# A two-block model in one kernel: the order of the even layer's mixers, their small operations, and where the modulation starts

## The chip, the cores and the metric

The kernel runs on one core of a Trainium2 chip, one launch. Times are device microseconds of that core. The time before is the median of three runs, 827.32 us (826.36 to 827.43). The engines are TensorE (PE; its weight loads are PEld), VectorE (DVE), ScalarE (ACT), GpSimd (POOL) and SyncE (SP), whose queue issues nearly all DMAs. TensorE's clock has two levels, 1.2 and 2.4 GHz; the profile shows the granted share of the higher.

## The reference

All tensors are float32; one sequence of 256 tokens, width 1024. The first block has two layers, x = x + layer(rms_norm(x)). The even one projects to mixers' columns, runs mLSTM (4 heads of 128) on one part and a sparse attention (8 heads of 64 in 2 groups) on the other, and projects back:

```python
proj = h @ w_in + b_in
ya = mlstm_branch(m_cols, ...)   # softmax-free attention with running gates, rms norm, * sigmoid(o) * silu(z)
yb = nsa_branch(n_cols, ...)     # (gated sum of compressed, selected and window attention) * silu(z)
return concatenate([ya, yb]) @ w_out
```

The odd layer is a gated recurrence (HGRN). The second block has a pooling layer and a spatial gating layer, each followed by an MLP of width 4096; every norm there is modulated by vectors that come from c:

```python
c_act = silu(c)
mod = c_act @ ada_w[i] + ada_b[i]          # 1024 x 6144, for each of two layers
sh1, sc1, g1, sh2, sc2, g2 = split(mod, 6)
h = rmsnorm(x, norm_mix_g[i]) * (1 + sc1) + sh1
```

## The kernel before

Activations lie transposed, features on partitions and the 256 tokens in the free dimension. Every large product is made at nearly fp32 accuracy from three fp32r matmuls: weights and activations are split into a high and a low part. Weights come by DMA as `raw` tiles of 128x2048 (1 MB, three buffers, two pieces of 1024 columns); `split_w` (L155 to L163) makes of a piece `whi`, a cast on ScalarE (L161), and `wlo`, a subtraction on VectorE (L162), four buffers each. `tile_T` (L190) then issues 24 matmuls (L221 to L223), eight k-steps of three; `tiles_tok` (L195; L206 to L208) is the same with tokens on the output's partitions and up to 512 columns. An output is evicted by `norm.scaled` (L310 to L313), a product with the norm's reciprocal root on VectorE, and what its kind wants.

The program is unrolled in Python. A scheduler puts each engine's instructions in order by priority, which is the place in the program, and by what it reckons to be ready; `tc.high_priority(offset=n)` moves an instruction's place n ahead, or back if n is negative. On the chip each engine keeps that order and waits at semaphores.

The even layer (`even_layer`, L404) works through 35 column tiles in the order of `EV_TILES` (L27): compress keys and values, the attention's keys and queries, gates G, values, then mLSTM's v, q and k, the gates mo, mz and nz. Between groups of tiles it advances two generators: `nsa` (L610: compress, query and key norms, then eight steps of attention, one per query block and head pair) and `mlstm` (L534: gates, four heads, a joint norm). The last attention step is run after mz3 and before nz0 (L527). Then out_proj (L315) runs eight tiles over the pairs `y` into xT. At L766 the attention's exponent takes scale 0.125 and a bias that L764 makes from the maximum.

An mLSTM head h spreads the rows `mr` and `bc` (4 heads by 256 tokens, fp32) over 128 partitions by a matmul with a one-hot column of the identity:

```python
sel = ident[0:4, h : h + 1].to_broadcast([4, 128])
PE.matmul(pb[:, 0:T], sel, mr, start=True, stop=False)
PE.matmul(pb[:, 0:128], ident_bf, mneg_bf, start=False, stop=True)
```

An fp32 matmul shows in the trace as two instructions.

`ada` (L340) makes the modulation vectors on VectorE: 96 loads of 128x1024 (`araw`, 512 KB, two buffers) and 96 reductions with the row c (L353). A step is one or two of them; `step(upto)` (L373) issues the next if fewer than 6 x upto are done, 50 places back in priority, so that they fill gaps. Before, steps start at L517 (`early`, in the mixers), at every second tile of the first out_proj (`every=2`), then in the odd layer and the MLPs; `finish` (L380) sets how many must be done at a point. silu of c is made at L509 to L512 by a tanh, after the first parts of nsa and mlstm, in an `araw` buffer.

`Norm.square` (L283) sums the squares of x over eight feature tiles on VectorE and adds over partitions by a ones-matmul; with `two` the eighth is given to a matmul of its own instead of the sum. Before, `two` holds where a norm has no shift.

Of the kernel before, what the change touches and what calls it, by code (L numbers as in the profile page):

```python
# [65 lines left out]
def tile_kernel(ctx: ExitStack, tc: tile.TileContext, io: dict, out: bass.AP):  # L66
# [82 lines left out]

    def load_raw(src, n=2048):  # L150
        raw = mk(wpool, [128, 2048], F32, "raw", bufs=3)
        nc.sync.dma_start(raw[:, :n], src)
        return raw

    def split_w(raw, piece, halves=False):  # L155

        hi = mk(wpool, [128, 1024], F32R, "whi", bufs=4)
        lo = mk(wpool, [128, 1024], F32R, "wlo", bufs=4)
        r = raw[:, piece * 1024 : (piece + 1) * 1024]
        for c in [slice(0, 1024)] if not halves else [slice(0, 512), slice(512, 1024)]:  # L160
            S.copy(hi[:, c], r[:, c])  # L161
            V.tensor_sub(lo[:, c], r[:, c], hi[:, c])  # L162
        return hi, lo  # L163
# [91 lines left out]
    class Norm:  # L255
# [3 lines left out]
        def __init__(self, gain=None, shift=None):  # L259
            self.gain, self.acc, self.ps, self.pair = gain, None, None, None  # L260
            if gain is not None:
                self.pair = Pair(0 if shift is None else 2)
            self.shift = shift
# [19 lines left out]
        def square(self, k, i=None):  # L283
            i = k if i is None else i
            sq = mk(tmp, [128, T], F32, "sq", bufs=3)
            S.activation(sq, xT[:, k, :], AF.Square)  # L286
            two = self.shift is None
            if i < KT - 1 or not two:
                if self.acc is not None:
                    V.tensor_tensor(sq, sq, self.acc, op=ALU.add)  # L290
                self.acc = sq
                if i < KT - 1 - two:
                    return
                self.ps = mbank()[:, :T]
# [20 lines left out]
    def out_proj(src, pair, evict, side=0, every=1):  # L315
        w = Weights(lambda c: src[c])
        for n in range(8):
            if every and n % every == 0:
                step(side)
            ps = gbank()[:, :T]  # L320
            tile_T(ps, w, n, pair)
            evict(n, ps)
# [81 lines left out]
    def even_layer(norm, nxt, w):  # L404
        with ExitStack() as es:
# [18 lines left out]
            def evict(name, ps):  # L424
# [25 lines left out]
                elif kind == "nz":  # L450

                    V.tensor_scalar(t, t, b, None, op0=ALU.add)
                    z = mk(et, [128, T], F32, "w1", bufs=4)
                    V.tensor_scalar(z, t, -80.0, None, op0=ALU.max)
# [3 lines left out]
                    V.tensor_tensor(nout[:, i, :], nout[:, i, :], t, op=ALU.mult)  # L458
# [43 lines left out]
            columns(EV_TILES[6:11])  # L502
# [5 lines left out]

            th = mk(wpool, [128, 1024], F32, "araw", bufs=2)  # L509
            tanh(th, crow, scale=0.5)  # L510
            V.scalar_tensor_tensor(crow, th, 1.0, crow, op0=ALU.add, op1=ALU.mult)
            V.tensor_scalar(crow, crow, 0.5, None, op0=ALU.mult)  # L512
            side.append(ada(crow))
# [18 lines left out]
            out_proj(io["ev_w_out"], y, add_x(nxt), 5, 2)  # L532

    def mlstm(ev, et, qk, v, gsb, num, tanh):  # L534
# [18 lines left out]
        V.tensor_scalar(mr, mr, -1.0, None, op0=ALU.mult)  # L553
        acol = mk(ev, [128, 2, H], F32, "acol")
# [7 lines left out]
        for h in range(H):  # L562
# [28 lines left out]
            PE.matmul(pm[:, 0:T], sel, bc, start=True, stop=True)  # L591
# [18 lines left out]
    def nsa(ev, et, nqk, sv, gsb, cpair, nout):  # L610
# [64 lines left out]
        gains = lambda i: P("q_norm") if i < 4 else P("k_norm", i - 3)  # L675
# [16 lines left out]
        V.memset(kcb, 0.0)  # L692
        for g in range(2):
            V.tensor_copy(kcb[64 * g : 64 * g + 64, g, :], kcmp[64 * g : 64 * g + 64, 0, :])

        hid4 = mk(et, [128, 2, 4, 32], F32, "w1", bufs=4)
        V.memset(hid4, 0.0)
        V.tensor_copy(hid4[:, :, :, 0:16], hid[:, 1, :, None, :].to_broadcast([128, 2, 4, 16]))
        vcp = mk(ev, [128, 2, 4, 64], F32, "vcp")
        V.memset(vcp, 0.0)  # L700
# [3 lines left out]
        for r in range(4):  # L704
            V.tensor_copy(vcp[32 * r : 32 * r + 32, :, r, :], ps[32 * r : 32 * r + 32, 0:128].rearrange("p (g e) -> p g e", g=2))
# [16 lines left out]
        for qb in range(2):  # L722
# [3 lines left out]
            mx = mk(et, [128, 4, 2, 2], F32, "nmx")  # L726
# [13 lines left out]
            V.memset(ec, 0.0)  # L740
            ecv = ec.rearrange("p g r n -> p (g r) n")[:, :, 0:15]
            V.tensor_tensor(ecv, pcv, mxc[:, :, None].to_broadcast([128, 8, 15]), op=ALU.subtract)
            S.activation(ecv, ecv, AF.Exp, scale=0.125)
# [12 lines left out]
            for j in range(4):  # L756
                E = mk(ev, [128, 2, 2, n], F32, "A", bufs=2)
                for g in range(2):
# [4 lines left out]
                    V.tensor_reduce(mx[:, j, g, :], pv, axis=AX.X, op=ALU.max)  # L763
                    V.tensor_scalar(nmx[:, j, g, :], mx[:, j, g, :], -0.125, None, op0=ALU.mult)  # L764
                    for b in range(2):
                        S.activation(E[:, g, b, :], pv[:, b, :], AF.Exp, bias=nmx[:, j, g, b : b + 1], scale=0.125,  # L766
# [415 lines left out]
    norm = Norm(mods[1][1][:, 0:8], mods[1][0][:, 0:8])  # L1182
    mlp(0, mod, mid, norm)
    mod, gains = mods[1]
    mid = Norm(gains[:, 8:16], mod[:, 24:32])
# [186 lines left out]
```

## Time and profile before

| | |
|---|---|
| median of three runs | 827.32 us |
| the profiled execution's own time | 825.35 us |
| its span, first to last instruction | 823.5 us |
| mean granted clock of TensorE | 0.99 |
| matmul, VectorE, ScalarE busy | 97%, 81%, 63% |
| instructions | 16419 |

The even layer lasts from the start to some 210 us of the span, the odd layer to about 350, the pool layer to about 372, the MLPs and the gating layer to the end. A busy share is the union of an engine's instructions; matmuls overlap in it. In the rows, "x4" is a count, "<-" names what ended a wait, and a line like L162 can be that of a helper used all over the program.

### The profile page before, as it was taken

The numbers are of one execution on the slowest core, as the hardware profiler recorded it, in microseconds if no ns is written. First come the engines' busy times: TensorE is split into PE (matmuls) and PEld (weight loads), VectorE is DVE, ScalarE is ACT, GpSimd is POOL, SyncE is SP. The second block draws the span as 40 slices with busy tenths as digits, with TensorE's granted clock in tenths as the row PEclk, the third lists the DMA queues.
The fourth block names the chain that finished last, engine by engine and source line by source line (L and its number), as shares of the span: only waits on it lengthen the run. The fifth ranks groups of instructions, "written<-read, shape, count | busy, mean of one in ns | idle before, by whom it ended". The sixth has DMA issues, their size and how long they took to land.

```text
span 823.5 us, 16419 instructions
## 1 busy us (share of the span) xinstructions
PE 802.5 (97%) x6568; PEld 739.9 (90%) x6568; DVE 670.8 (81%) x1260; ACT 519.7 (63%) x932; POOL 4.9 (1%) x19
## 2 busy tenths in 40 slices
PE   8999999998999999998999999999999999999996
PEld 7969987888999987998999988889999999988885
DVE  7689988899999999998999988756679877755552
ACT  6656765686876565756877734446657877754441
POOL 0000000001000000000000000000000000000000
PEclk8999999999999999999999999999999999999999
DMA  9644566657885677747989888654446655555521
GB/s 353 244 165 148 179 215 229 228 191 258 301 288 214 245 253 262 232 174 284 345 283 320 304 294 310 245 201 154 168 152 234 221 199 166 193 190 174 199 103 52
DMA packets 34636, 184.66 MB, mean 224 GB/s; under 512 B 3968, under 2 KB 4608, under 8 KB 19200
## 3 DMA queue, kind: packets, MB, share of 16 engines
q1 hardware_dynamic: 33696, 181.96, 62.8%
q10 hardware_dynamic: 864, 1.65, 0.6%
q8 instruction: 52, 0.85, 0.4%
q14 instruction: 24, 0.20, 0.1%
HBM read 182.55 MB, written 1.05 MB: 223 GB/s over the span
## 4 chain that ended last, share of the span: by engine, by line
PE 68%; DVE 15%; DMA 8%; ACT 4%; issue 4%; ACTq 0%; DVEq 0%; SPq 0%
PE g L221 13%; PE g L223 12%; PE g L222 12%; PE g L1057 10%; DMA araw<-in_ada_w_dram 7%; DVE wlo L162 5%; PE g L1058 5%; DVE araw L353 3%; PE m L871 1%; ACT whi L161 1%; PE m L761 1%; DVE nt L312 1%; PE g L207 1%; PE g L208 1%; PE g L206 1%
## 5 line engine op out<-in xcount | busy, mean ns | idle before, releaser
L221 PE MATMUL g<-ahi,whi 128*128 128x258 f32 (+1 forms) x1256 | 359.3, 288 | 8.1 <-ACT ahi L213 3.3
L222 PE MATMUL g<-alo,whi 128*128 128x258 f32 (+1 forms) x1256 | 357.5, 286 | 0.1
L223 PE MATMUL g<-ahi,wlo 128*128 128x258 f32 (+1 forms) x1256 | 356.7, 285 | 0.3 <-DVE wlo L162 0.2
L162 DVE TENSOR_TENSOR wlo<-raw,whi 128x1024 fp32r<-128x1024 f32 (+1 forms) x238 | 288.7, 1216 | 79.9 <-ACT whi L161 79.2
L161 ACT CAST whi<-raw 128x1024 fp32r<-128x1024 f32 (+1 forms) x238 | 246.5, 1043 | 166.8 <-PE g L222 67.0
L221 PEld LDWEIGHTS g<-ahi,whi 128*128 128x128 f32 x1256 | 238.7, 191 | 12.7 <-ACT ahi L213 4.1
L222 PEld LDWEIGHTS g<-alo,whi 128*128 128x128 f32 x1256 | 240.0, 191 | 2.1 <-issue 0.8
L223 PEld LDWEIGHTS g<-ahi,wlo 128*128 128x128 f32 x1256 | 239.3, 191 | 2.1 <-issue 1.0
L1057 PE MATMUL g<-ghl,whi 128*128 128x512 f32 x480 | 168.2, 393 | 0.0
L353 DVE CUSTOM_DVE_ANT_0 araw<-araw,row_c,prm 128x1024 f32<-128x1024 f32 x96 | 122.4, 1278 | 18.0 <-DMA araw<-in_ada_w_dram 17.9
L1058 PE MATMUL g<-ghl,wlo 128*128 128x256 f32 x480 | 134.1, 279 | 0.6 <-DVE wlo L162 0.6
L1057 PEld LDWEIGHTS g<-ghl,whi 128*128 128x128 f32 x480 | 89.9, 187 | 21.2
L1058 PEld LDWEIGHTS g<-ghl,wlo 128*128 128x128 f32 x480 | 89.9, 187 | 1.2 <-DVE wlo L162 1.2
L312 DVE TENSOR_TENSOR nt<-g,nrstd 128x256 f32<-128x256 f32 x133 | 55.5, 418 | 15.1 <-PE g L223 14.3
L1039 ACT ACTIVATE nt<-nt,nb 128x256 f32<-128x256 f32 x64 | 32.4, 507 | 23.5 <-DVE nb L1038 23.5
L280 ACT ACTIVATE ahi<-xT,gains 128x256 fp32r<-128x256 f32 x32 | 16.2, 505 | 23.6 <-DVE xT L332 22.2
L286 ACT ACTIVATE sq<-xT 128x256 f32<-128x256 f32 x56 | 22.3, 404 | 10.6 <-DVE xT L332 10.6
L214 DVE TENSOR_TENSOR ghl<-nt,ghl 128x256 fp32r<-128x256 f32 x64 | 26.9, 422 | 2.2 <-ACT ghl L213 0.2
L1040 ACT ACTIVATE nt<-nt 128x256 f32<-128x256 f32 x64 | 26.7, 418 | 1.9
L213 ACT CAST ghl<-nt 128x256 fp32r<-128x256 f32 x64 | 25.9, 406 | 1.8
L208 PE MATMUL g<-wlo,ahi 128*128 128x512 f32 (+1 forms) x64 | 24.3, 379 | 0.0
L206 PE MATMUL g<-whi,ahi 128*128 128x512 f32 (+1 forms) x64 | 24.2, 378 | 0.0
(302 smaller groups left out, 803.1 us busy)
## 6 DMA issues: line engine op xcount, KB each, us to landing
raw<-in_mlp_w_dram SPq DMA_DIRECT2D x64, 1024.0 KB, 5.0
araw<-in_ada_w_dram SPq DMA_DIRECT2D x96, 512.0 KB, 4.9
raw<-in_ev_w_in_dram SPq DMA_DIRECT2D x17, 1024.0 KB, 5.5
raw<-in_od_w_in_dram SPq DMA_DIRECT2D x16, 1024.0 KB, 5.2
raw<-in_sgu_w_in_dram SPq DMA_DIRECT2D x8, 1024.0 KB, 4.9
raw<-in_ev_w_out_dram SPq DMA_DIRECT2D x4, 1024.0 KB, 4.9
raw<-in_od_w_out_dram SPq DMA_DIRECT2D x4, 1024.0 KB, 4.8
raw<-in_sgu_w_out_dram SPq DMA_DIRECT2D x4, 1024.0 KB, 4.8
```

The source lines that it names most:

```text
L161: S.copy(hi[:, c], r[:, c])
L162: V.tensor_sub(lo[:, c], r[:, c], hi[:, c])
L206: PE.matmul(ps[tb], pair.hi(k)[:, ts_], wh[:, j, :], start=st, stop=False)
L208: PE.matmul(ps[tb], pair.hi(k)[:, ts_], wl[:, j, :], start=False, stop=sp)
L221: PE.matmul(ps, wh(k), ah(k), start=st, stop=False)
L222: PE.matmul(ps, wh(k), al(k), start=False, stop=False)
L223: PE.matmul(ps, wl(k), ah(k), start=False, stop=sp)
L312: V.tensor_tensor(t, ps[:, :T], self.r, op=ALU.mult)
L353: V.tensor_tensor_reduce(raw, raw, crow, 1.0, P("ada_b", layer * 48 + c), ALU.mult, ALU.add, mod[:, c : c + 1])
L1039: S.activation(r, r, AF.Relu, bias=b)
L1057: PE.matmul(ps, wh[:, k, :], a.rearrange("p s t -> p (s t)"), start=st, stop=sp, skip_group_check=True)
L1058: PE.matmul(ps[:, :T], wl[:, k, :], a[:, 0, :], start=False, stop=sp, skip_group_check=True)
```

## The change

Splits of weights get 80 places of priority from the seventh tile of the even layer to the end of its out_proj (`lead`). silu of c is made by exp, ln and exp right before the seventh tile, and one ada step follows each of the tiles 7 to 11. out_proj's steps move to n = 3, 5, 7. The last attention step is run after mo3, ahead of mz0. In mLSTM the rows are split into a high and a low fp32r part in one tile `rows` (partitions 0 to 3 and 32 to 35), and a stationary `two` adds both; the 256 and the 128 columns of `mr` become one product of 384, the two masks one of 256. In the attention the 0.125 goes into the query gain, the negation into the reduction; memsets go from VectorE to GpSimd and small copies from VectorE to ScalarE. nz saves one VectorE operation. The pool layer's second norm is now one with `two`.

```diff
+    lead = [0]
@@ split_w
-        for c in [slice(0, 1024)] if not halves else [slice(0, 512), slice(512, 1024)]:
-            S.copy(hi[:, c], r[:, c])
-            V.tensor_sub(lo[:, c], r[:, c], hi[:, c])
+        with tc.high_priority(offset=lead[0]):
+            for c in [slice(0, 1024)] if not halves else [slice(0, 512), slice(512, 1024)]:
+                S.copy(hi[:, c], r[:, c])
+                V.tensor_sub(lo[:, c], r[:, c], hi[:, c])
@@ Norm
-        def __init__(self, gain=None, shift=None):
+        def __init__(self, gain=None, shift=None, two=True):
...
-            two = self.shift is None
+            two = self.two
@@ out_proj
-            if every and n % every == 0:
+            if every and n % every == every - 1 and n > 1:
                 step(side)
@@ evict, nz
-                    V.tensor_scalar(t, t, b, None, op0=ALU.add)
                     z = mk(et, [128, T], F32, "w1", bufs=4)
-                    V.tensor_scalar(z, t, -80.0, None, op0=ALU.max)
+                    V.tensor_scalar(z, t, b, -80.0, op0=ALU.add, op1=ALU.max)
...
-                    V.tensor_tensor(nout[:, i, :], nout[:, i, :], t, op=ALU.mult)
+                    V.scalar_tensor_tensor(nout[:, i, :], t, b, nout[:, i, :], op0=ALU.add, op1=ALU.mult)
@@ even_layer
             crow = bcast_rows(base, "c")
-            columns(EV_TILES[6:11])
+            lead[0] = 80
+
+            th = mk(wpool, [128, 1024], F32, "araw", bufs=2)
+            V.tensor_scalar(th, crow, -80.0, None, op0=ALU.max)
+            tab[0].activation(th, th, AF.Exp, scale=-1.0)
+            tab[0].activation(th, th, AF.Ln, bias=1.0)
+            tab[0].activation(th, th, AF.Exp, scale=-1.0)
+            V.tensor_tensor(crow, crow, th, op=ALU.mult)
+            side.append(ada(crow))
+            for name in EV_TILES[6:11]:
+                columns([name])
+                step(1)
...
-            th = mk(wpool, [128, 1024], F32, "araw", bufs=2)
-            tanh(th, crow, scale=0.5)
-            V.scalar_tensor_tensor(crow, th, 1.0, crow, op0=ALU.add, op1=ALU.mult)
-            V.tensor_scalar(crow, crow, 0.5, None, op0=ALU.mult)
-            side.append(ada(crow))
...
-            columns(EV_TILES[25:31])
+            columns(EV_TILES[25:27])
+            run(ns)
+            columns(EV_TILES[27:31])
             tab[0] = Table(EXP_LN, tab[0])
             run(ml)
-            run(ns)
...
             out_proj(io["ev_w_out"], y, add_x(nxt), 5, 2)
+            lead[0] = 0
@@ mlstm
+        rows = mk(ev, [128, 640], F32R, "rows")
+        G.memset(rows.bitcast(U32), 0)
+        for c, r in ((slice(0, 256), mr), (slice(256, 384), mr[:, 128:256]), (slice(384, 640), bc)):
+            S.copy(rows[0:4, c], r)
+            V.tensor_sub(rows[32:36, c], r, rows[0:4, c])
+        two = mk(ev, [128, H], F32R, "two")
+        V.tensor_tensor(two, ident[:, 0:4], ident[:, 32:36], op=ALU.add)
...
-            sel = ident[0:4, h : h + 1].to_broadcast([4, 128])
+            sel = two[:, h : h + 1].to_broadcast([128, 128])
             pb = mbank(1)
-            PE.matmul(pb[:, 0:T], sel, mr, start=True, stop=False)
-            PE.matmul(pb[:, 0:128], ident_bf, mneg_bf, start=False, stop=True)
-            PE.matmul(pb[:, 256:384], sel, mr[:, 128:256], start=True, stop=False)
-            PE.matmul(pb[:, 256:384], ident_bf, mneg_bf, start=False, stop=True)
+            PE.matmul(pb[:, 0:384], sel, rows[:, 0:384], start=True, stop=False, skip_group_check=True)
+            diag = pb.rearrange("p (s t) -> p s t", s=2)[:, :, 0:128]
+            PE.matmul(diag, ident_bf, mneg_bf[:, None, :].to_broadcast([128, 2, 128]), start=False, stop=True, skip_group_check=True)
...
-            PE.matmul(pm[:, 0:T], sel, bc, start=True, stop=True)
+            PE.matmul(pm[:, 0:T], sel, rows[:, 384:640], start=True, stop=True)
@@ nsa
+        qg = mk(ev, [128, 1], F32, "qgain")
+        S.mul(qg, P("q_norm"), 0.125)
...
-        V.memset(kblk, 0.0)
+        G.memset(kblk, 0.0)
         for g in range(2):
-            V.tensor_copy(kblk[64 * g : 64 * g + 64, g, :, :], nqk[64 * g : 64 * g + 64, 4:6, :])
+            S.copy(kblk[64 * g : 64 * g + 64, g, :, :], nqk[64 * g : 64 * g + 64, 4:6, :])
...
-                    V.tensor_reduce(mx[:, j, g, :], pv, axis=AX.X, op=ALU.max)
-                    V.tensor_scalar(nmx[:, j, g, :], mx[:, j, g, :], -0.125, None, op0=ALU.mult)
+                    V.tensor_reduce(nmx[:, j, g, :], pv, axis=AX.X, op=ALU.max, negate=True)
```

Left out are the same moves for `kcb`, `hid4`, `vcp` and `ec` (memsets to GpSimd; the copies into `kcb` and `vcp` to ScalarE), the scale 0.125 gone from both exponents, and `False` for `two` written at the gating layer's two norms, which keeps them as they were.

## Rows read from the trace of the kernel before

**Rows 1.** the page, part 1: busy time, share of the span, instructions

```profile
PE 802.5 (97%) x6568; PEld 739.9 (90%) x6568; DVE 670.8 (81%) x1260; ACT 519.7 (63%) x932; POOL 4.9 (1%) x19
```

**Rows 2.** windows: stretch, length, busy us by engine, granted clock, DMA share, GB/s

```profile
29.00:54.00 25.00, 23.60 (x211) 20.04 (x210) 16.32 (x30) 11.93 (x19) 0.53 (x1) 1.00 0.69 249
...
73.00:76.00 3.00, 2.95 (x18) 2.12 (x18) 3.00 (x11) 2.39 (x6) 0.00 (x0) 1.00 0.00 0
76.00:79.50 3.50, 3.50 (x19) 3.50 (x18) 3.50 (x9) 1.54 (x5) 0.20 (x2) 0.51 0.77 279
...
106.00:145.00 39.00, 39.00 (x246) 30.65 (x245) 33.31 (x78) 23.06 (x73) 0.00 (x0) 1.00 0.69 227
...
173.00:196.00 23.00, 19.46 (x150) 17.45 (x149) 20.92 (x50) 14.75 (x36) 2.71 (x2) 1.00 0.59 191
...
373.00:381.00 8.00, 5.82 (x35) 5.62 (x35) 4.67 (x10) 5.63 (x11) 0.00 (x0) 0.79 0.91 345
```

**Rows 3.** chain of waits: start us, us (for matmuls, time TensorE is held), what

```profile
53.96 0.24 PE g L207
...
107.61 0.11 PE m L762
...
109.57 0.62 PE m L591 x2
...
110.63 0.12 PE g L223
...
112.19 0.62 PE m L570 x2
112.81 0.16 PE m L571
112.98 0.41 PE m L572 x2
113.39 0.16 PE m L573
...
352.48 0.12 PE m L994
```

**Rows 4.** the chain of waits at the even layer's end

```profile
184.67 0.76 DVE nout L458 x2
...
188.00 1.19 DVE araw L353
...
192.91 1.11 DVE araw L353
194.16 0.34 DVE xT L326
194.54 0.38 PE g L221
```

**Rows 5.** lines of the span, then 73 to 173 and 29 to 73 us

```profile
L353 DVE CUSTOM_DVE_ANT_0 araw<-araw,row_c,prm 128x1024 f32<-128x1024 f32 x96 | 122.4, 1278 | 18.0 <-DMA araw<-in_ada_w_dram 17.9
...
L764 DVE TENSOR_SCALAR nnmx<-nmx 128x2 f32<-128x2 f32 x16 | 2.6, 161 | 0.0
...
L161 ACT CAST whi<-raw 128x1024 fp32r<-128x1024 f32 x17 | 17.8, 1047 | 9.1 <-PE g L222 9.1
...
L511 DVE SCALAR_TENSOR_TENSOR row_c<-araw,row_c 128x1024 f32<-128x1024 f32 x1 | 1.2, 1222 | 0.0
```

**Rows 6.** timeline of SP and VectorE: start us, us, engine, line, operation

```profile
37.38 23.24 SPq L152 DMA_DIRECT2D raw<-in_ev_w_in_dram  x5
...
42.23 0.48 DVE L478 SCALAR_TENSOR_TENSOR sv<-g,rcol,row_sv 128x256 f32<-128x256 f32 x1 [3.46 <-DMA raw<-in_ev_w_in_dram]
...
95.62 1.28 DVE L353 CUSTOM_DVE_ANT_0 araw<-araw,row_c,prm 128x1024 f32<-128x1024 f32 x1
```

**Rows 7.** the chain of waits after the pool layer

```profile
370.89 9.09 DMA araw<-in_ada_w_dram
```

**Rows 8.** waits of ScalarE in 73 to 173 us: total us, times, longest us

```profile
ACT whi L161 <- PE g L222: 9.1, 7, 3.8
```

More of the change, by code (lines that the diff above doesn't have):

```diff
@@ L262, in __init__ @@
                 self.pair = Pair(0 if shift is None else 2)
-            self.shift = shift
+            self.shift, self.two = shift, two
         def feed(self, k, i=None):
@@ L674, in nsa @@
         V.tensor_tensor(hid.rearrange("p c g n -> p (c g n)"), x_, u_, op=ALU.mult)
-        gains = lambda i: P("q_norm") if i < 4 else P("k_norm", i - 3)
+        qg = mk(ev, [128, 1], F32, "qgain")
+        S.mul(qg, P("q_norm"), 0.125)
+        gains = lambda i: qg if i < 4 else P("k_norm", i - 3)
         for i0, m in ((4, 2), (0, 4)):
@@ L691, in nsa @@
         kcb = mk(ev, [128, 2, 15], F32, "kcb")
-        V.memset(kcb, 0.0)
+        G.memset(kcb, 0.0)
         for g in range(2):
-            V.tensor_copy(kcb[64 * g : 64 * g + 64, g, :], kcmp[64 * g : 64 * g + 64, 0, :])
+            S.copy(kcb[64 * g : 64 * g + 64, g, :], kcmp[64 * g : 64 * g + 64, 0, :])
         hid4 = mk(et, [128, 2, 4, 32], F32, "w1", bufs=4)
-        V.memset(hid4, 0.0)
+        G.memset(hid4, 0.0)
         V.tensor_copy(hid4[:, :, :, 0:16], hid[:, 1, :, None, :].to_broadcast([128, 2, 4, 16]))
         vcp = mk(ev, [128, 2, 4, 64], F32, "vcp")
-        V.memset(vcp, 0.0)
+        G.memset(vcp, 0.0)
         ps = mbank(0)
@@ L704, in nsa @@
         for r in range(4):
-            V.tensor_copy(vcp[32 * r : 32 * r + 32, :, r, :], ps[32 * r : 32 * r + 32, 0:128].rearrange("p (g e) -> p g e", g=2))
+            S.copy(vcp[32 * r : 32 * r + 32, :, r, :], ps[32 * r : 32 * r + 32, 0:128].rearrange("p (g e) -> p g e", g=2))
         gtok = mk(ev, [128, 2, 24], F32, "gtok")
@@ L724, in nsa @@
             qs = slice(qb * 128, qb * 128 + 128)
-            mx = mk(et, [128, 4, 2, 2], F32, "nmx")
             nmx = mk(et, [128, 4, 2, 2], F32, "nnmx")
@@ L739, in nsa @@
             ec = mk(et, [128, 2, 4, 32], F32, "nEc")
-            V.memset(ec, 0.0)
+            G.memset(ec, 0.0)
             ecv = ec.rearrange("p g r n -> p (g r) n")[:, :, 0:15]
             V.tensor_tensor(ecv, pcv, mxc[:, :, None].to_broadcast([128, 8, 15]), op=ALU.subtract)
-            S.activation(ecv, ecv, AF.Exp, scale=0.125)
+            S.activation(ecv, ecv, AF.Exp)
             V.tensor_reduce(smc, ecv, axis=AX.X, op=ALU.add)
@@ L762, in nsa @@
                     PE.matmul(pv[:, :, n - 128 : n], ident_bf, nneg_bf[:, None, :].to_broadcast([128, 2, 128]), start=False, stop=True)
-                    V.tensor_reduce(mx[:, j, g, :], pv, axis=AX.X, op=ALU.max)
-                    V.tensor_scalar(nmx[:, j, g, :], mx[:, j, g, :], -0.125, None, op0=ALU.mult)
+                    V.tensor_reduce(nmx[:, j, g, :], pv, axis=AX.X, op=ALU.max, negate=True)
                     for b in range(2):
-                        S.activation(E[:, g, b, :], pv[:, b, :], AF.Exp, bias=nmx[:, j, g, b : b + 1], scale=0.125,
+                        S.activation(E[:, g, b, :], pv[:, b, :], AF.Exp, bias=nmx[:, j, g, b : b + 1],
                                      accum_out=sm[:, j, g, b : b + 1])
@@ L1181, in tile_kernel @@
     consts = sgu_consts(ctx.enter_context(tc.tile_pool(name="sc", bufs=1)))
-    norm = Norm(mods[1][1][:, 0:8], mods[1][0][:, 0:8])
+    norm = Norm(mods[1][1][:, 0:8], mods[1][0][:, 0:8], False)
     mlp(0, mod, mid, norm)
     mod, gains = mods[1]
-    mid = Norm(gains[:, 8:16], mod[:, 24:32])
+    mid = Norm(gains[:, 8:16], mod[:, 24:32], False)
     sgu_layer(consts, mod, gains, norm, mid)
```

## The prediction, made before the change was run

> **What bounds the kernel now.** I read the page first: over the whole span TensorE's matmul rows are busy 802.5 of 823.5 us, VectorE 670.8 [rows 1]. So an edit pays where it removes matmul time, or where it fills one of the few places in which TensorE idles. The stage windows come next, because the diff touches only the even layer, its c, and one norm of the pool layer [rows 2]. In 106 to 145 us, where three of the four mLSTM heads run between projection tiles, TensorE is busy 39.00 of 39.00 us and VectorE 33.31: the length of that stretch is its matmul work. In 29 to 54 us TensorE idles 25.00 - 23.60 = 1.4 us and in 173 to 196 us 23.00 - 19.46 = 3.5 us. In 76 to 79.5 us the granted clock is 0.51, the lower of its two levels (1.2 GHz); TensorE lost half of 3.5 us there, some 1.7 us. In the 3 us before that fall VectorE was busy 3.00 of 3.00 us and TensorE ran short matmuls of the mixers. After 214 us nothing but the order of the ada work and the pool layer's second norm changes. Last, the chain of waits: it gives, in stretches without idle, the time that each matmul holds TensorE, which is not its duration in the groups, since those overlap.
>
> **mLSTM matmuls (the one term that is sure).** Per head the kernel issues fp32 matmuls with 4 rows: the chain has L591 as two pieces in 0.62 us, L570 two in 0.62, L572 two in 0.41, and the bf16 masks L571 and L573 at 0.16 each [rows 3], together 1.97 us. The change issues three instead. The 384-column fp32r product is in no row; the 512-column one holds TensorE 0.24 us and the 256-column one 0.12 [rows 3], so it lies between, and by columns I take 0.18. Its stationary is a broadcast column; L994, fp32r with a broadcast stationary, holds 0.12 for 256 columns [rows 3], so that adds nothing. The joined mask is bf16 with 256 columns, as L762: 0.11. The bcum product is fp32r with 256 columns: 0.12. Sum 0.41, saving 1.56 a head, **6.2 us** for four. Between ends: with 0.24 for the new product 6.0, with 0.12 it is 6.5. Three heads lie where TensorE is always busy, so theirs counts whole; the first starts in the stretch where VectorE was the fuller engine [rows 2], so at the least 4.7 us are seen. To feed these matmuls the change adds once a memset on GpSimd, three copies on ScalarE, four subtractions or additions on VectorE, each over 4 rows of 256 columns or less, for which I take the 0.38 us of a 128x256 product (nout L458, two in 0.76) [rows 4] as an upper bound: some 1.5 us on either engine before the first head's exponent. Projection tiles cover it; uncovered, the first head starts 3 us later and nothing after it does.
>
> **VectorE's relief.** Taken off VectorE: sixteen negations L764, 2.6 us [rows 5]; also the copies into kblk, kcb and vcp, a memset, and one operation per nz tile. The copies go to ScalarE, busy 23.06 of 39.00 us in the middle stretch [rows 2]. The 0.125 moves into the query gain: one small multiply. The memsets go to GpSimd's queue, idle but for a wait on the compress tile; all but one run as soon as the program starts. None of it counts by itself, since VectorE is not the bound at 106 to 145 us. It counts in the 3 us before the clock fell: with the silu of c gone from there too (L511 alone 1.2 us [rows 5]) VectorE hands the weight split over earlier, and the fall at 76 us may not come. Ends: 1.7 us gained, or another fall elsewhere, 1.7 lost; I take **0.9 us gained**, nearer to the gain because the 4-row matmuls ahead of it are gone.
>
> **Silu of c and five ada steps earlier.** Exp, ln, exp replace tanh: two more 128x1024 passes on ScalarE, 1.0 us each as the cast L161 [rows 5], by the table that is loaded there. They move ahead of the seventh tile; ScalarE's 25.00 - 11.93 = 13.1 us of slack in 29 to 54 us [rows 2] covers them. The five steps after tiles 7 to 11 are seven loads of 512 KB on SP's queue and seven VectorE reductions of 1.28 us [rows 5]: 9.0 us of VectorE and 3.5 MB. Before, the first such reduction ran at 95.6 us [rows 6]. VectorE is idle 25.00 - 16.32 = 8.7 us of the stretch 29 to 54 [rows 2], which is room for nearly all. But the loads share the DMA engines with the weight load issued at 37.38, whose landing VectorE awaited for 3.46 us [rows 6], with projection, compress and key norm behind it, and a reduction at the head of VectorE's queue holds the splits behind it. At the best the earlier silu and the lighter queue recover the stage's 1.4 us; at the worst one load lands as the one at 370.89, after 9.09 us [rows 7], where TensorE idled 8.00 - 5.82 = 2.2 us and the clock fell for 1.7 more [rows 2], 3.9 together. I take **1.5 us lost**, between the two and nearer to the first, because VectorE and ScalarE have that slack.
>
> **Attention's last step ahead of mz, and steps off out_proj's first tiles.** The end of the layer is a chain: nout from 184.67 us by way of gate, split and two ada reductions at 188.00 and 192.91 (1.19 and 1.11 us of it) to the first released accumulator at 194.16 and TensorE at 194.54 [rows 4]. With the attention finished four tiles sooner, the chain starts at the last nz tile: scale, max, three ScalarE passes, two products, cast, difference, nine pieces of 0.38 us, 3.4 us, and out_proj's first seven k-steps stand ready to cover part of it. Ada reductions may still slip in, since the trace shows them filling gaps wherever they stand in the program. Of the 3.5 us idle I take **2.5 us gained**, ends 0 and 3.5.
>
> **Splits ahead.** No instruction is added; costed at 0 in the sum. In 73 to 173 us ScalarE waited before a split for TensorE to free a buffer 7 times, 9.1 us, at most 3.8 [rows 8]: four buffers, not priority, set how far splits can lead, and what comes behind such a wait is covered as long as ScalarE has 39.00 - 23.06 us to spare. The rule that speaks against this edit stands by itself: the Trainium skill, TensorE: Matmul & The Clock Gate, section on the architectural detail of the array, says that ScalarE and VectorE take their queues strictly in order. The trace agrees: during the waits of [rows 8] ScalarE ran nothing else. By it a split that is put forward and then waits would hold the mixers' exponents; that is the second case below.
>
> **Pool norm.** One VectorE sum leaves the end of a chain and one fp32 ones-product comes: within 0.4 us either way, 0.
>
> **The sum.** 6.2 + 0.9 - 1.5 + 2.5 = 8.1 us saved, against the profiled execution's own 825.35 us: 817.2. That execution lies 1.97 us under the median of the three runs, 827.32, so the median I forecast is 827.32 - 8.1 = **819.2 us**.
>
> **Rivals.**
> *Splits hold the queue.* If the other ten of the seventeen splits of 73 to 173 us [rows 5] wait too, at the mean 9.1 / 7 = 1.3 us [rows 8], the mixers' ScalarE work runs 13 us later. The attention gained four tiles, 4 x 24 x 0.12 = 11.5 us [rows 3], so it ends 1.5 us late, the tail's 2.5 and the clock's 0.9 are gone: 6.2 - 1.5 - 1.5 = 3.2 saved, 824.1. For it: the waits exist already. Against: ScalarE's slack.
> *All relief is kept.* 6.2 + 3.5 + 1.7 + 1.4 = 12.8, 814.5. For it: every idle place named has its cause removed. Against: seven more loads in the stage that waits for a load.
> *Slower: early ada loads starve the weights.* Place: 29 to 73 us. Price 3.9 us a stall, as at 373 to 381 us [rows 2, 7]. Against other gains of 6.2 + 2.5 + 0.9 = 9.6 it decides from the third stall: 3 x 3.9 - 9.6 = 2.1 lost, 829.4. For it: the loads there have two buffers and one queue with the weights. Against: DMA share 0.69 in 29 to 54 us [rows 2].
> *The relief doesn't reach the clock on the wall.* If VectorE were the bound of the mixers, the matmul saving would turn into idle: 827.3. Against: 33.31 of 39.00.
>
> **How the numbers follow.** Forecast 0.50, queue 0.19, all relief 0.18, starved weights 0.09, no effect 0.04. About 0.2%, 1.65 us, is what a measurement of this kernel can tell. Faster: the first and third whole, most of the second, 0.82. Same: the last and the edges of second and fourth, 0.10. Slower 0.08. The forecast's own ends, from 4.7 + 0.9 - 1.5 + 0 = 4.1 saved to 6.5 + 1.7 + 3.5 = 11.7, are 815.6 to 823.2; adding the second case, most of the third and a little of the fourth gives 812.5 to 826.5.
>
> **What would show it.** Right: the pieces of the three new products near 0.18, 0.11 and 0.12 us; TensorE's idle between the last nz tile and the first out_proj tile near 1 us; no fall of the clock before 100 us; the first ada reduction before 50 us. Wrong: a ScalarE wait before splits over 20 us in the mixers (second case); VectorE waiting on ada loads for several us before 73 us (fourth); new products at 0.3 us or more, which breaks the first term.

## The result, and the profile of the changed kernel

The changed kernel takes **813.36 us** (median of four runs, 812.67 to 814.34) where the kernel before takes 826.84 beside it (824.84 to 827.43): a ratio of 0.9846 (95% interval 0.9825 to 0.9866), 13.5 us faster. The forecast was 819.2 with a range of 812.5 to 826.5. The direction and the range held; the gain is 5 us larger than the sum of 8.1. The profiled execution took 813.74 us, its span is 812.0, its mean granted clock 0.998.

The page's part 1 answers to [rows 1]: matmul rows 12.0 us less busy, VectorE 6.8 less, ScalarE 5.0 more, with the share of TensorE as it was.

```profile
PE 790.5 (97%) x6550; PEld 732.8 (90%) x6550; DVE 664.0 (82%) x1229; ACT 524.7 (65%) x946; POOL 7.6 (1%) x26
```

The windows answer to [rows 2], with the same columns (stretch, length, busy of TensorE, its weight loads, VectorE, ScalarE, GpSimd, granted clock, DMA share, GB/s):

```profile
29.00:54.00 25.00, 22.95 (x214) 20.70 (x213) 20.12 (x37) 12.28 (x19) 0.78 (x2) 1.00 0.84 291
...
76.00:79.50 3.50, 3.28 (x27) 2.98 (x26) 3.44 (x11) 3.21 (x6) 0.10 (x1) 1.00 0.21 87
106.00:145.00 39.00, 39.00 (x278) 33.18 (x276) 35.58 (x77) 28.63 (x87) 0.00 (x0) 1.00 0.71 242
...
164.00:184.00 20.00, 19.44 (x161) 18.34 (x160) 19.31 (x44) 14.93 (x37) 2.54 (x2) 1.00 0.33 117
...
220.00:245.00 25.00, 21.60 (x462) 20.37 (x461) 23.34 (x38) 17.72 (x29) 0.00 (x0) 1.00 0.79 271
373.00:381.00 8.00, 8.00 (x69) 8.00 (x69) 8.00 (x16) 6.13 (x12) 0.00 (x0) 1.00 0.93 327
```

Four things are to be seen. In this execution the fall of the clock at 76 us is gone. TensorE is busy all through 373 to 381 us, but the program is some 10 us ahead there; in the place that answers to it, 363 to 371 us, TensorE idles 1.3 us where it idled 2.2, at a granted clock of 1.00:

```profile
363.00:371.00 8.00, 6.72 (x55) 6.49 (x54) 6.57 (x15) 5.73 (x11) 0.00 (x0) 1.00 0.91 350
```

In 29 to 54 us TensorE idles 2.05 us, where it idled 1.4: VectorE is 3.8 us busier there, with ada reductions. The layer's end, 164 to 184 us, has 0.6 us of idle left. And a new hole of 3.4 us stands in the odd layer, at 220 to 245.

The chain of waits at the even layer's end answers to [rows 4]: the attention's last output is copied at 173.36 us, two ada reductions are left in the chain (one cut short by overlap), and the first released accumulator lets TensorE go on at 182.86, against 194.54.

```profile
173.36 0.60 ACT nout L812
173.98 0.88 DVE nout L461 x2
...
179.73 1.20 DVE araw L357
180.93 0.34 DVE alo L218
181.27 0.63 DVE araw L357
181.90 0.49 issue
182.47 0.34 DVE xT L330
182.86 0.39 PE g L225
```

The timeline of TensorE at an mLSTM head answers to [rows 3] (start us, us, line, operation, tile): the 384-column product starts 0.17 us before the joined mask, the mask 0.06 before a projection matmul.

```profile
78.55 0.33 PE L589 MATMUL m<-rows,two 128*128 128x384 f32 x1
78.72 0.28 PE L591 MATMUL m<-mnegbf,identbf 128*128 128x256 bf16 x1
78.78 0.38 PE L225 MATMUL g<-ahi,whi 128*128 128x256 f32 x1
```

The chain of waits has the time that the other two new products hold TensorE, at the second head:

```profile
111.66 0.12 PE m L591
...
117.74 0.12 PE m L609
```

The timeline of VectorE answers to [rows 6]: ada reductions run from 36.34 us, and two waits for their loads show (2.55 and 0.66 us). The line after them, from the waits of ScalarE in 73 to 173 us, answers to [rows 8]: 4.7 us in 6 waits, where it was 9.1 in 7.

```profile
36.34 1.27 DVE L357 CUSTOM_DVE_ANT_0 araw<-araw,row_c,prm 128x1024 f32<-128x1024 f32 x1
...
43.11 1.28 DVE L357 CUSTOM_DVE_ANT_0 araw<-araw,row_c,prm 128x1024 f32<-128x1024 f32 x1 [2.55 <-DMA araw<-in_ada_w_dram]
...
56.96 1.29 DVE L357 CUSTOM_DVE_ANT_0 araw<-araw,row_c,prm 128x1024 f32<-128x1024 f32 x1 [0.66 <-DMA araw<-in_ada_w_dram]
```

```profile
ACT whi L165 <- PE g L226: 4.7, 6, 1.4
```

### The profile page after: what moved, and what is told of

Same layout as the page of the kernel before. It is cut to its first block, busy times and chain, and to the rows that moved or that the text cites. A ratio compares the mean times of both kernels' runs of the same rounds, so it can differ in the third digit from the quotient of the medians.

```text
span 812.0 us, 16365 instructions
## 1 busy us (share of the span) xinstructions
PE 790.5 (97%) x6550; PEld 732.8 (90%) x6550; DVE 664.0 (82%) x1229; ACT 524.7 (65%) x946; POOL 7.6 (1%) x26
## 4 chain that ended last, share of the span: by engine, by line
PE 78%; DVE 10%; ACT 5%; DMA 4%; issue 2%; ACTq 0%; DVEq 0%
PE g L225 15%; PE g L226 15%; PE g L227 15%; PE g L1076 14%; PE g L1077 7%; DVE wlo L166 3%; DMA araw<-in_ada_w_dram 3%; DVE araw L357 2%; PE m L890 2%; ACT whi L165 1%; PE m L781 1%; PE long L808 1%; PE g L210 1%; PE g L211 1%; PE g L212 1%
## 5 line engine op out<-in xcount | busy, mean ns | idle before, releaser
L211 PE MATMUL g<-whi,alo 128*128 128x512 f32 (+1 forms) x64 | 24.4, 382 | 0.0
```

The costliest lines, as they stand in the source:

```text
L211: PE.matmul(ps[tb], pair.lo(k)[:, ts_], wh[:, j, :], start=False, stop=False)
```

## The experiments

Each ratio below is to the kernel before on the same chip, and "us" beside it is that ratio's distance from 1 times 825 us, the median of before in those runs. By this measure the whole change gains 12.7 us.

| kernel | median us | ratio (95%) | us |
|---|---|---|---|
| changed kernel | 813.36 | 0.9846 (0.9825 to 0.9866) | -12.7 |
| before + mLSTM rows | 829.34 | 1.0047 (1.0021 to 1.0072) | +3.9 |
| before + rows + order | 829.0 | 1.0047 (1.0018 to 1.0075) | +3.9 |
| before + rows + lead | 822.76 | 0.9982 (0.9962 to 1.0002) | -1.5 |
| before + rows + order + lead | 821.91 | 0.9958 (0.9944 to 0.9973) | -3.5 |
| changed, rows as before | 821.44 | 0.9953 (0.9930 to 0.9975) | -3.9 |
| changed, no lead | 821.73 | 0.9941 (0.9915 to 0.9967) | -4.9 |
| changed, attention late | 822.96 | 0.9959 (0.9934 to 0.9984) | -3.4 |
| changed, silu late | 819.35 | 0.9925 (0.9895 to 0.9955) | -6.2 |
| changed, relief undone | 820.05 | 0.9934 (0.9909 to 0.9959) | -5.4 |
| changed, out_proj's steps as before | 813.98 | 0.9856 (0.9822 to 0.9891) | -11.9 |
| changed, pool norm as before | 814.58 | 0.9860 (0.9826 to 0.9894) | -11.6 |
| changed, lead to the end | 815.22 | 0.9891 (0.9864 to 0.9918) | -9.0 |

A second table is worked out from the traces of the profiled executions. It gives when ScalarE copied the attention's last output (`nout<-long`), how many ada reductions began between 165 and 200 us, and how much later (+) or sooner than before TensorE started the last column tile of the mixers (174.8 us before), the fourth tile of out_proj (194.5) and the odd layer's second tile (213.4), and ended the span (823.5). The last two columns are TensorE's idle time in 164 to 205 us, and how many column tiles its order still holds when the first product of the attention's last step (`m<-kblk,nqk`) has its turn.

| kernel | last output us | ada 165-200 | last tile | out_proj 4th | odd 2nd | span | idle us | tiles left |
|---|---|---|---|---|---|---|---|---|
| before | 184.05 | 6 | 0 | 0 | 0 | 0 | 3.65 | 1.5 |
| before + rows | 184.46 | 7 | -8.5 | +2.5 | +4.0 | +3.6 | 7.25 | 0 |
| + order | 185.29 | 7 | -7.6 | +3.6 | +6.3 | +6.1 | 7.68 | 0 |
| + lead | 174.90 | 5 | -8.0 | -8.5 | -7.1 | -5.0 | 3.67 | 1.5 |
| + order + lead | 175.53 | 5 | -7.0 | -7.8 | -7.0 | -4.7 | 2.96 | 1.3 |
| changed, rows as before | 177.93 | 4 | +4.6 | -2.1 | -0.5 | -1.0 | 1.51 | 3.1 |
| changed, no lead | 174.89 | 5 | -6.2 | -8.3 | -6.8 | -8.2 | 2.32 | 1.4 |
| changed, attention late | 175.68 | 6 | -7.0 | -5.8 | -3.8 | -2.9 | 4.48 | 1.3 |
| changed, silu late | 174.70 | 4 | -6.1 | -7.7 | -6.3 | -4.3 | 2.91 | 1.6 |
| changed, relief undone | 179.14 | 5 | -4.1 | -5.0 | -5.0 | -6.4 | 2.91 | 1.5 |
| changed | 173.36 | 3 | -7.3 | -11.7 | -11.8 | -11.5 | 0.58 | 2.0 |
| changed, out_proj's steps as before | 173.49 | 3 | -7.2 | -11.5 | -11.6 | -9.2 | 0.58 | 2.0 |
| changed, pool norm as before | 174.18 | 3 | -6.5 | -10.9 | -10.9 | -9.4 | 0.57 | 2.0 |
| changed, lead to the end | 176.66 | 2 | -4.0 | -8.4 | -8.5 | -3.6 | 0.65 | 2.0 |

Each row is one execution. The last three kernels run the changed kernel's instructions in the same order up to 191 us or beyond, so the last four rows show how far executions of one program lie apart: 3.3 us in the last output, the last tile and the fourth tile of out_proj. "Before + rows" and "+ order" are one program too: every engine has the same instructions in the same order to the end. A smaller difference between two rows shows nothing by itself. Some profiled executions lie far from their median: that of "no lead" took 817.05 (median 821.73), of "rows as before" 824.22 (821.44), of "silu late" 822.55 (819.35), of "lead to the end" 822.33 (815.22).

**The rows alone.** The mLSTM hunk of the diff put into the kernel before.

```diff
-            PE.matmul(pb[:, 0:T], sel, mr, start=True, stop=False)
...
+            PE.matmul(pb[:, 0:384], sel, rows[:, 0:384], start=True, stop=False, skip_group_check=True)
...
-            PE.matmul(pm[:, 0:T], sel, bc, start=True, stop=True)
+            PE.matmul(pm[:, 0:T], sel, rows[:, 384:640], start=True, stop=True)
```

> The kernel before with one part of the change, the mLSTM rows in fp32r (three matmuls a head for the eight pieces). If TensorE bounds the mixers: 6.2 us faster than before, 5 to 7, and the new pieces hold TensorE 0.18, 0.11 and 0.12 us. If VectorE or the order of the queues bounds them: under 3 us faster, with the saved matmul time found as idle between 100 and 150 us.

It came out 3.9 us slower than before: the term that was called sure costs time when it stands alone. Neither case above came true: TensorE idles only 0.05 us in 100 to 150 us. The trace shows two other places. The first is at 76 to 81 us. The timeline of ScalarE (first line) and VectorE:

```profile
64.08 1.05 ACT L161 CAST whi<-raw 128x1024 fp32r<-128x1024 f32 x1 [0.76 <-PE g L207]
...
66.27 1.22 DVE L162 TENSOR_TENSOR wlo<-raw,whi 128x1024 fp32r<-128x1024 f32 x1
...
75.56 0.41 DVE L312 TENSOR_TENSOR nt<-g,nrstd 128x256 f32<-128x256 f32 x1
76.05 1.22 DVE L511 SCALAR_TENSOR_TENSOR row_c<-araw,row_c 128x1024 f32<-128x1024 f32 x1
77.19 0.48 DVE L440 SCALAR_TENSOR_TENSOR qk<-mqk,prm,qk 128x256 f32<-128x256 f32 x1
77.59 0.68 DVE L512 TENSOR_SCALAR row_c<-row_c 128x1024 f32<-128x1024 f32 x1
...
79.71 1.21 DVE L162 TENSOR_TENSOR wlo<-raw,whi 128x1024 fp32r<-128x1024 f32 x1
```

and the next line of TensorE, with the stretch around it by the windows (columns as above):

```profile
80.98 0.38 PE L223 MATMUL g<-ahi,wlo 128*128 128x256 f32 x1 [4.45 <-DVE wlo L162]
```

```profile
76.00:81.00 5.00, 0.55 (x4) 0.32 (x3) 4.95 (x11) 4.17 (x11) 0.10 (x1) 1.00 0.35 107
78.00:84.00 6.00, 3.02 (x11) 2.21 (x12) 6.00 (x13) 2.54 (x7) 0.20 (x2) 0.79 0.41 105
```

TensorE, with its matmuls gone, came to the weights sooner and stood 4.45 us for one split, the twentieth of the program. The twentieth cast had started on ScalarE at 64.08 us, so the split's input was long there; but VectorE ran no split between 66.27 and 79.71 us. It worked off the silu of c and small sums first, one after the other, and the clock fell behind the wait. A second kernel with the same instructions (rows and order, below) shows the wait again, 4.46 us. It didn't make the attention start late: its first step's products start at 81.5 us, where they started at 83.3 before. The second place is the layer's end, by the chain of waits:

```profile
180.43 0.59 ACT nPT L792
181.07 2.03 PE long L797 x10
...
184.46 0.59 ACT nout L801
...
188.18 1.19 DVE araw L353
...
189.98 1.19 DVE araw L353
191.21 4.13 DMA araw<-in_ada_w_dram
195.37 1.28 DVE araw L353
...
197.05 0.39 PE g L221
```

TensorE began its last column tile 8.5 us sooner, and the attention's last output still came at 184.46 (184.05 before). So TensorE ran out of projection tiles before the attention ended. Its order shows why: in the kernel before, 1.5 column tiles stand behind the first product of the attention's last step, here none. The edit touches no line that places them; this order is the scheduler's. TensorE was busy 17.10 of 20 and 16.65 of 21 us in 164 to 205, at granted clocks of 0.91 and 0.84, where the kernel before has 19.40 and 17.95 and the changed one 19.44 and 20.98, both at 1.00; three ada reductions and a load of 4.13 us stood in what followed. The windows of 184 to 205 us, before and changed:

```profile
184.00:205.00 21.00, 17.95 (x143) 17.13 (x143) 19.46 (x45) 13.88 (x27) 2.71 (x2) 1.00 0.74 259
184.00:205.00 21.00, 20.98 (x171) 20.37 (x170) 20.34 (x45) 16.21 (x31) 0.17 (x1) 1.00 0.86 306
```

**The changed kernel with the rows as before.**

```diff
+            PE.matmul(pb[:, 0:T], sel, mr, start=True, stop=False)
...
-            PE.matmul(pm[:, 0:T], sel, rows[:, 384:640], start=True, stop=True)
+            PE.matmul(pm[:, 0:T], sel, bc, start=True, stop=True)
```

> The changed kernel with the old mLSTM matmuls, so everything else of the change: 13.5 - 6.2 = 7.3 us faster than before if the two add up. If the rest only works because TensorE is relieved, less than 4 us faster; if the fp32r rows are not what pays, more than 10 us faster.

It loses 8.8 of the 12.7 us. In this company the rows are worth more than their own 6.2 us; by the second table its mixers end 4.6 us later than before, not earlier. That is one execution, the slowest of ten, in which the granted clock was 0.87 in 29 to 54 us, so the table overstates it; most of this loss lies in the mixers and not at the layer's end.

**The splits' lead taken away.**

```diff
-            lead[0] = 80
+            lead[0] = 0
```

> The changed kernel with the 80 places of priority taken from the splits. Theory: four buffers bound how far splits can lead, so the lead is worth nothing: 13.5 us faster than before, within 1.5. Rival: the lead keeps TensorE fed in the mixers, and without it 3 to 5 us of the gain go. Second rival, the strict queues: the lead holds the mixers' exponents, and without it the kernel is 1 to 3 us faster still.

7.8 us lost, where the prediction had 0 and the rival 3 to 5. Its profiled execution is the shortest of its ten, so the trace shows only a part of that: five ada reductions in the layer's end instead of three, 1.4 tiles left instead of 2.0, 1.7 us less of TensorE busy in 184 to 205 us and a granted clock of 0.92 there. And TensorE stood 3.03 us for one split, which VectorE ran at 57.91 us behind an ada reduction and small operations:

```profile
57.91 2.34 DVE L166 TENSOR_TENSOR wlo<-raw,whi 128x1024 fp32r<-128x1024 f32 x2
59.17 0.50 PE L212 MATMUL g<-wlo,ahi 128*128 128x512 f32 x1 [3.03 <-DVE wlo L166]
```

**The attention's last step back behind mz.**

```diff
-            columns(EV_TILES[25:27])
-            run(ns)
-            columns(EV_TILES[27:31])
+            columns(EV_TILES[25:31])
             tab[0] = Table(EXP_LN, tab[0])
             run(ml)
+            run(ns)
```

> The changed kernel with attention's last step back behind mz and ahead of nz. Theory: the even layer's end gained about 4.3 us from this move, so 9 to 10 us faster than before and TensorE idle of 3 us or more between the last nz tile and the first out_proj tile. Rival: the ada steps taken off out_proj's first tiles did it, and the move is worth under 1 us.

9.3 us lost, the largest of all, where 4.3 was expected. The last output is only 2.3 us later, within what executions of one program differ by, but 1.3 tiles are left instead of 2.0 and six ada reductions stand in the end of the layer; TensorE is busy 17.98 of 20 and 18.54 of 21 us there, at a granted clock of 0.84 in the second stretch.

**The silu of c by tanh at its old place, no early ada steps.**

```diff
-            for name in EV_TILES[6:11]:
-                columns([name])
-                step(1)
+            columns(EV_TILES[6:11])
...
+            tanh(th, crow, scale=0.5)
```

> The changed kernel with silu of c by tanh at its old place and without the five early ada steps. Theory: the early place costs some 2.3 us of TensorE idle in 29 to 73 us and saves the 1.7 us of the clock's fall at 76 us, so the kernel stays 13.5 us faster than before, within 1.5, and the idle of 29 to 54 us is back at 1.4 us. If the relief of VectorE ahead of the heads is worth more, 10 us faster; if the early loads only cost, 15 to 16.

6.5 us lost. At 68.8 us of the kernel before, the changed kernel is 1.4 us behind it (1.1 to 2.9 in the four executions of that program) and this one 0.1: the local loss is near what the prediction had. But at the odd layer's second tile this one has gained 6.3 us and the changed kernel 11.8. By counts of ada reductions begun, 20 have begun at 202 us here, 25 in the changed kernel. How the early ones come to save time at the layer's end isn't shown.

**Out_proj's steps and the pool norm as before**, two kernels with one line each.

```diff
-            if every and n % every == every - 1 and n > 1:
+            if every and n % every == 0:
```

> The changed kernel with the ada steps of the two out_proj at their old tiles, 0, 2, 4 and 6 in the first. Theory: the scheduler fills gaps with ada work wherever it stands, so no difference: 13.5 us faster, within 1. Rival: two reductions come back into the chain at the layer's end, 2 to 3 us less gain.

```diff
-        mid = Norm(gains[:, 8:16], mod[:, 24:32])
+        mid = Norm(gains[:, 8:16], mod[:, 24:32], False)
```

> The changed kernel with the pool layer's second norm as before, eight sums and one ones-matmul. Theory: 13.5 us faster than before, within 0.5, since the chain is shorter by 0.3 us at most. Rival: the early hand-over moves the ada loads behind it and so spares the clock's fall at 376 us of the kernel before; without it that fall is back and 1.5 us of the gain go.

Both lie within the interval of the changed kernel. Neither edit does anything that stands clear of the noise here, some 2 us.

**VectorE's relief undone** in the attention and in nz: negation, copies, memsets and the extra operation back on VectorE.

```diff
-                    V.tensor_reduce(nmx[:, j, g, :], pv, axis=AX.X, op=ALU.max, negate=True)
+                    V.tensor_reduce(mx[:, j, g, :], pv, axis=AX.X, op=ALU.max)
+                    V.tensor_scalar(nmx[:, j, g, :], mx[:, j, g, :], -0.125, None, op0=ALU.mult)
```

> The changed kernel with the attention's small work as before: negations, memsets and copies on VectorE, scale 0.125 in the exponent, and the extra nz operation. Theory: VectorE does not bound the mixers, so 12.5 to 13.5 us faster than before. Rival: VectorE, busy 34.59 of 37.00 us in 100 to 137 us of the changed kernel, is next in line, and 3 us or more of the gain go.

7.3 us lost, where some 1 was expected. The last output comes at 179.14 us, later than in any of the four executions with the relief (173.36 to 176.66), and 1.5 tiles are left instead of 2.0. That fits small operations of VectorE that pace the attention's steps, though VectorE was busy only 33.31 of 39.00 us in 106 to 145 us before [rows 2]. Which of them pays, and where, wasn't separated.

**The parts put together again**, on the kernel before with the rows: order alone, lead alone, both.

```diff
+            columns(EV_TILES[25:27])
+            run(ns)
+            columns(EV_TILES[27:31])
```

> The kernel before with the mLSTM products and the attention's last step ahead of mz0, nothing else. Rows alone lost 3.9 us. Theory A, each part has a worth of its own (order 8 to 9 us by the run that put it back, rows as measured alone): 4 to 6 us faster than before. Theory B, the layer's end has several limits one behind the other, and the attention's chain was the first of them: the loss of the rows alone goes, but ada reductions and splits are next, so 1 us slower to 3 us faster, with TensorE still idle over 3 us between the last nz tile and out_proj.

```diff
+            lead[0] = 80
             columns(EV_TILES[6:11])
```

> The kernel before with the mLSTM products and the splits 80 places ahead, nothing else. Theory A (lead 7 us, rows alone 3.9 lost): 3 us faster than before. Theory B: the attention still ends behind mz, so early splits give TensorE nothing that it may start: as the rows alone, 2 to 5 us slower than before.

> The kernel before with the mLSTM products, the attention's last step ahead of mz0 and the splits ahead; the silu, the early ada steps, the relief of VectorE and the rest as before. Theory A: 11 us faster or more, as the whole change. Theory B: the first two limits are gone, the ada reductions and VectorE's small work remain: 4 to 8 us faster.

Both theories missed the order alone. It changes nothing (1.0047 again), and the traces say why: the scheduler gave every engine the same instructions in the same order as with the rows alone. So this run says nothing of what the move is worth on the chip; it says that a move in the program need not be one in the schedule. From the attention's first step to its last TensorE works through 16.75 column tiles in both. The lead alone brings back 5.4 us; theory A's 3 us faster lies at the edge of its interval, theory B is refuted. It is the lead that pulls the attention forward here, to 174.90: between the two steps TensorE now has 13.25 column tiles, 3.5 fewer.

```profile
174.90 0.59 ACT L806 COPY nout<-long 128x512 f32<-128x512 f32 x1 [0.91 <-PE long L803]
```

The timeline of VectorE shows what else it does, at the place where TensorE stood 4.45 us with the rows alone: the twentieth split runs at 76.41 us, right behind the silu and ahead of most of the small sums, and no longer at 79.71; two more stand close to it.

```profile
72.81 1.22 DVE L165 TENSOR_TENSOR wlo<-raw,whi 128x1024 fp32r<-128x1024 f32 x1
...
74.34 1.22 DVE L515 SCALAR_TENSOR_TENSOR row_c<-araw,row_c 128x1024 f32<-128x1024 f32 x1
...
76.41 1.22 DVE L165 TENSOR_TENSOR wlo<-raw,whi 128x1024 fp32r<-128x1024 f32 x1
...
79.10 1.23 DVE L165 TENSOR_TENSOR wlo<-raw,whi 128x1024 fp32r<-128x1024 f32 x1
```

```profile
76.00:81.00 5.00, 4.51 (x38) 4.28 (x37) 5.00 (x10) 3.22 (x6) 0.10 (x1) 1.00 0.72 272
```

In that stretch TensorE was busy 4.51 of 5.00 us, against 0.55. With order and lead the kernel is 3.5 us faster than before, just under the band of 4 to 8 expected. From there to the whole change 9.2 us are missing; relief without the silu brings 2.7 of them (-6.2 to -3.5), the silu without relief 1.9, the two together all. Steps of 2 to 3 us here are no larger than the intervals.

**The lead kept to the program's end.**

```diff
             out_proj(io["ev_w_out"], y, add_x(nxt), 5, 2)
-            lead[0] = 0
```

> The changed kernel with the splits 80 places ahead to the program's end and not only to the even layer's. If splits late behind ada reductions are what the odd layer gives back between 220 and 245 us (3.4 us of idle) and what the pool layer idles, 2 to 4 us faster than the changed kernel; if the ada loads themselves hold VectorE there (a wait of 6.01 us in the chain at 218 us), no change within 1 us; if splits put forward wait for buffers in front of VectorE's own chain in the recurrence, 1 to 4 us slower than the changed kernel.

Not faster: 0.9891, 3.7 us behind the changed kernel by its ratio, 1.9 by the medians; the two intervals touch. So late splits aren't shown to make the hole of the odd layer, and 2.6 us of it are left here. In the changed kernel 1.8 us of TensorE's waits there are for the recurrence's own operands; the last, 1.56 us, ends with nothing that the profile shows:

```profile
226.47 0.33 PE L890 MATMUL m<-hq,hk 128*32 128x32 f32 x16 [1.21 <-ACT hq L397]
230.07 0.76 PE L890 MATMUL m<-hq,hk 128*32 128x32 f32 x64 [0.23 <-DVE hq L932]
234.28 0.70 PE L890 MATMUL m<-hq,hk 128*32 128x32 f32 x56 [0.39 <-DVE hk L939]
236.53 0.27 PE L890 MATMUL m<-hq,hk 128*32 128x32 f32 x8 [1.56 <-issue]
```

Each kernel that reaches the odd layer 6 us or more early gives back 1.3 to 4.3 us between its second tile and the tile that the kernel before starts at 244.8 us (the changed one 3.7): what is late next lies in the recurrence.

## Why the prediction was right, and where it was wrong

The direction and the range were right; that the sum came as near as it did is in part luck, for errors of both signs are in it. 813.36 lies outside the forecast's own ends, 815.6 to 823.2; the range holds because the rival in which all relief is kept, 814.5, was taken into it. That rival's sum isn't borne out either: of its four terms the idle time of 29 to 54 us was not regained (2.05 us, 1.4 before), and its sure term, the rows, costs time alone.

**mLSTM matmuls.** The prices held: the three new products were taken as 0.18, 0.11 and 0.12 us, and the chain has them at 0.17 or 0.18, 0.12 or 0.13, and 0.12. But the step that failed is the sentence behind them, "three heads lie where TensorE is always busy, so theirs counts whole", and with it the reading that the term is sure. Alone, the rows cost 3.9 us. A full TensorE at 106 to 145 us shows that TensorE bounds that stretch; it doesn't show that the stretch behind it starts sooner. The attention, on ScalarE and VectorE, ended at 184 us in both kernels, and the time saved came back as idle at the layer's end, 7.25 us where it was 3.65. The rival "no effect", at a chance of 0.04, said that the matmul saving would turn into idle; for the rows alone that is what happened, though not for the reason that it gave.

**VectorE's relief.** "None of it counts by itself" failed. Taken away, it costs 7.3 us. The clock at 76 us, for which 0.9 was counted, stayed up in the profiled execution; but in two of the three other executions of the same instructions it fell close by (72 to 76 us, with the pool norm as before and with the lead to the end), so this term isn't shown.

```profile
72.00:76.00 4.00, 4.00 (x26) 3.81 (x25) 3.19 (x12) 2.38 (x8) 0.00 (x0) 0.71 0.63 203
72.00:76.00 4.00, 4.00 (x23) 4.00 (x23) 3.20 (x10) 2.57 (x9) 0.00 (x0) 0.58 0.15 31
```

That VectorE was busy 33.31 of 39.00 us in the middle of the mixers [rows 2] was read as slack that makes the relief worth nothing; the run says otherwise.

**Silu of c and early steps.** 1.5 us lost was right for its place (1.1 to 2.9 at 68.8 us in four executions, 2.55 and 0.66 us of waits for loads). What was missed is what it pays later: without it the kernel is 6.5 us slower.

**Attention ahead of mz.** 2.5 us gained was the term; taken out of the changed kernel it costs 9.3, beside the rows and the lead it brings 2.0, and beside the rows alone it left the schedule as it was. The chain's start did move, from 184.05 to 173.36 us, but not by this edit alone: with the rows it is the lead that moves it, and the changed kernel without this edit has 175.68. The prediction's "four tiles sooner" took the place in the program for the place in TensorE's order, where 2.0 tiles are left behind the step, and 1.5 before.

**Splits ahead.** Costed at 0; the lead is worth 5.4 us beside the rows alone and 7.8 in the changed kernel. The prediction looked at ScalarE, where a split put forward may wait. The rows show waits on VectorE: with the rows alone a split behind 1.22 and 0.68 us of silu and a row of small sums held TensorE for 4.45 us, and without the lead in the changed kernel one held it for 3.03. With it the longest such wait in the first 100 us is 1.1 us or less. The rule itself stands in the Trainium skill, TensorE: Matmul & The Clock Gate, section on the architectural detail of the array: ScalarE and VectorE take their queues strictly in order. These rows agree with it; the prediction weighed it for ScalarE, and on VectorE it speaks for the edit. ScalarE's waits before splits fell from 9.1 us [rows 8] to 4.7, and the lead taken away costs time, so the rival of splits that hold the queue is refuted. For the rival of starved weights there are 3.2 us of waits by VectorE for ada loads in the first 100 us, and no idle TensorE of the price that it needs.

**Pool norm and out_proj's steps.** 0 fits both, within some 2 us.

What the runs show in place of the sum: five edits, each worth 6.5 to 9.3 us when it is the one left out, 39.7 us together, for a gain of 12.7. So the terms don't add. The second table says where much of this lies. TensorE goes through its instructions in the order that the scheduler made, and each edit changes that order: how many column tiles are left to run while the attention's last step passes through ScalarE and VectorE. With none left TensorE idles 7.3 to 7.7 us in 164 to 205 us, with 1.3 to 1.6 left 2.3 to 4.5, with 2.0 left 0.6 in all four executions. The kernel with the old rows has 3.1 left and idles 1.5; it loses its time earlier. So an edit pays in full only if the others leave enough work there. This is read off the orders of the traces; no run set the number of tiles by itself. The fall of the clock (granted 0.76 to 0.92 in 184 to 205 us in seven of the nine incomplete kernels, 1.00 in the changed one) adds to the miss in those seven.

Four things are open. Why the scheduler makes these orders isn't known. Why five or more ada reductions fall into 165 to 200 us in most of the incomplete kernels and two or three in the whole one isn't known either, and a kernel that holds them out of that stretch wasn't tried. And of the 7.8 us of the lead in the changed kernel, the one profiled execution, 3.3 us longer than the changed kernel's, can explain under half. Last, no part but the rows was put into the kernel before by itself; the lead, which does most there, was tried only beside the rows.

## What to carry to other kernels

Before a saving on the busiest engine is called sure, follow what ends the stage behind it: if another chain ends there at a time of its own, the saving is idle time until that chain is shortened too. Where a scheduler orders the engines, read that order again after every edit: here the rows alone took the tiles left behind the attention's last step from 1.5 to none. Work that fills gaps must stand behind, in the queue, whatever the busiest engine waits for next. To judge a bundle of edits, leave each out of the whole and also put it in alone, and see in the trace that the schedule did change; here the two answers differ by 12.7 us for the one edit that has both (the rows, +3.9 alone and -8.8 in company).

## What the runs showed of the hardware that was not expected

An edit whose main effect is to take work from TensorE can lower its clock: with the rows alone the mean granted clock was 0.980 to 0.989 in ten executions, with a mean of 0.986 (0.981 to 0.989 in six more of the same instructions), where the kernel before has 0.986 to 0.996 in 31, with a mean of 0.992. In the profiled execution it was 0.79 in 78 to 84 us, behind 4.45 us of waiting, and 0.84 in 184 to 205, where the kernel before has 1.00 in that last stretch; before, it fell earlier, to 0.51 in 76 to 79.5 us.

An fp32r product of 384 columns with a broadcast stationary holds TensorE 0.17 us, where the two 4-row fp32 products that it replaces held 0.62 and 0.41 [rows 3]. Few rows made those no cheaper: in the same chain of waits an fp32 product of 256 columns over 128 rows (L585) holds TensorE 0.43 us, the 4-row one of 256 columns 0.62.
